# Four direct pairs in every feed-forward, and groups of seven products begun earlier

## The chip, the cores and the metric

The kernel runs on one core of one Trainium2 chip (trn2). The metric is the device time of one execution in microseconds (us), as the median of several runs. The engines of a core run side by side, each with its own queue in order: TensorE (PE in the profile, with PEld for its weight loads) does the matrix products, VectorE (DVE) and ScalarE (ACT) do the elementwise work, GpSimd (POOL) here issues the transfers that add while they write, and SyncE (SP) issues the plain transfers.

## The reference

Two decoder layers over 512 tokens of width 1024, all in float32. Each layer has three residual parts, and the change lies in the first and third:

```python
def swiglu_ffn(x, g, w_in, w_out):
    h = rms_norm(x, g)
    gate, up = jnp.split(h @ w_in, 2, axis=-1)
    return (jax.nn.silu(gate) * up) @ w_out
...
    for layer in range(DEPTH):
        x = x + 0.5 * swiglu_ffn(x, ffn1_norm[layer], ffn1_w_in[layer], ffn1_w_out[layer])
        # layer 0: retention and dilated attention; layer 1: stick-breaking attention
        ...
        x = x + 0.5 * swiglu_ffn(x, ffn2_norm[layer], ffn2_w_in[layer], ffn2_w_out[layer])
    return rms_norm(x, final_norm)
```

`D_FF` is 2816, so `w_in` has 22 column blocks of 128 for the gate and 22 for the up half, and `w_out` has 22 row blocks. There are four feed-forwards, called FFN0 to FFN3 below.

## The kernel before

**Precision.** A float32 product is made of three products of the short type fp32r. Every operand is split into `hi`, its rounded value, and `lo`, what is left. Then `hi*hi`, `hi*lo` and `lo*hi` are added up in PSUM. `split` (L224) makes the two with one ScalarE cast (L225) and one VectorE subtraction (L226). Where the source still lies in device memory there is a second way: ScalarE writes `-hi` into the `lo` buffer, and a transfer from POOL's queue adds the source to it. It is `weight_dma` (L194, with `minus_hi`, L189, its transfer is L192) for direct weights, and `cut_raw` (L468; cast L471, negation L472, transfer L473) for the blocks of a group.

**Two ways to do the first product.** A feed-forward's 22 gate and up blocks are done partly in *direct pairs* and partly in *groups of seven products*. A direct pair is one gate and one up block: 48 matmuls with 512 columns (8 row blocks, three fp32r products, gate and up). A group covers two gate and two up blocks by Winograd's form of Strassen's scheme: seven products of half the rows and half the tokens where the plain way needs eight. Each product is 24 matmuls with 256 columns. How many pairs are direct is `DIRECT`, one number for each feed-forward (L32); before, it is 6, 4, 4, 6, and the rest are 8, 9, 9 and 8 groups. `lazy` (L547) is true where it is 4: then the direct weights from the third pair on take `weight_dma`, the token forms are made one by one as the groups ask for them (a Python generator, `normed_forms`, L420), and buffers are dealt out differently.

**A group** is `quad` (L493). It loads four blocks a21, a11, a22, a12 of 512 KB (L497). The weight side of its products is, in order: p3, the sum of a11 and a21 (L499); p1, an addition in a21's buffer (L507); a22; a11; p2, an addition in a22's buffer (L513); p4, an addition in a11's buffer (L517); a12. The token sides are the forms T3, T1, T4, B11, T2, B22 and B21. Products T3 and T4 go into one PSUM bank one after the other, T1 and B22 into a second, B11 and B21 into a third, T2 into a fourth. Between T3 and T4 ScalarE has to copy the bank out (L505). The evictions after T2 are L522, L524 and L526, after B22 the addition L529, a silu and a product (L533), after B21 another silu and L533.

**Buffers.** Tiles come from numbered slots that are handed out in the order of the program, each role in a ring. While the groups run, the loaded blocks (`wraw`) have 7 slots for 4 blocks a group, the splits (`whl`) have 10 slots, that is five products' `hi` and `lo`, and p3 has one. So the split of a product can begin when the product five places ahead of it in the ring has been done. The first group of a feed-forward inherits the slots of the direct pairs in the order in which those were used.

**Order.** TensorE's instructions keep the order of the program by explicit edges (`ordered`, L119). The other engines' orders are laid out ahead by a scheduler that walks through modelled time: whenever an engine is free it takes, of the instructions that are ready in that model, the one written earliest. Once laid out, each queue runs strictly in order on the chip. So where a piece of code stands in the program decides which slots it gets and who goes first when two are ready.

**Around it.** Ahead of the direct pairs the norm's scale is finished by `norm_r` and `rstd` (ln and exp on ScalarE, then three VectorE instructions, L244, L245, L247), and everything that comes after the direct products needs it: the evictions of the pairs (L580, L587, L590), the normed activations (L429), their sums (L446) and the splits of the forms (L225 and L226). After the groups comes the second product (`out_ffn` or `out_last`).

Of the kernel before, what the change touches and what calls it, by code (L numbers as in the profile page):

```python
# [25 lines left out]
FC = DFF // P  # L26
# [2 lines left out]
NEG = -1.0e30  # L29
NORM_EPS = 1e-6  # L30
GN_EPS = 1e-5
DIRECT = (6, 4, 4, 6)  # L32


@with_exitstack
def trunk(ctx: ExitStack, tc: tile.TileContext, a: dict, out: bass.AP):
    nc = tc.nc
# [24 lines left out]
    def others():  # L62

        return [i for i in range(10, NSLOT) if i not in home["h"]]
# [13 lines left out]
    def B(shape, dt, tag):  # L78
        slot = roles[tag][turn_of[tag] % len(roles[tag])]
        turn_of[tag] += 1  # L80
        return big.tile(list(shape), dt, tag=f"m{slot}", name=nm(tag), bufs=1)
# [7 lines left out]
    def ATT():  # L89
        return PS("att")  # L90

    def f32(ap):
        return ap.bitcast(F32)
# [31 lines left out]
    def mm(*args, **kw):  # L125
        return ordered(nc.tensor.matmul(*args, **kw))  # L126
# [97 lines left out]
    def split(hi, lo, src):  # L224
        nc.scalar.copy(out=hi, in_=src)  # L225
        nc.vector.tensor_tensor(out=lo, in0=src, in1=f32(hi), op=ALU.subtract)  # L226
# [241 lines left out]
    def cut_raw(raw, src):  # L468

        hi, lo = (B((P, 2, SEQ), F32R, "whl") for _ in range(2))  # L470
        nc.scalar.copy(out=hi, in_=raw)  # L471
        nc.scalar.mul(out=lo, in_=f32(hi), mul=-1.0)  # L472
        nc.gpsimd.dma_start(lo, src, accum_op=ALU.add)  # L473
        return hi, lo

    def cut_form(src):
        hi, lo = (B((P, 2, SEQ), F32R, "whl") for _ in range(2))
        split(hi, lo, src)
        return hi, lo

    def product(bank, w, form, first):

        for p in range(2):
            o = bank[:, p * HT:p * HT + HT]
            for k in range(4):
                col = slice(k * P, k * P + P)
                h, l = (t[:, p, col] for t in w)
                bh, bl = form[k // 2][:, 0, k % 2, :], form[k // 2][:, 1, k % 2, :]
                mm(o, h, bh, start=first and p == 0 and k == 0, stop=False, skip_group_check=True)
                mm(o, h, bl, start=False, stop=False, skip_group_check=True)  # L490
                mm(o, l, bh, start=False, stop=k == 3, skip_group_check=True)

    def quad(wq, fm, uq, early, lazy):  # L493

        a21, a11, a22, a12 = (B((P, 2, SEQ), F32, "wraw") for _ in range(4))
        for t, i in ((a21, 2), (a11, 0), (a22, 3), (a12, 1)):
            nc.sync.dma_start(t, wq[i])  # L497
        p3 = B((P, 2, SEQ), F32, "p3")
        nc.vector.tensor_add(out=p3, in0=a11, in1=a21)  # L499
        if early and lazy:  # L500
            w22 = cut_raw(a22, wq[3])
        bc, bd_, ba, bb = (ATT() for _ in range(4))
        product(bc, cut_form(p3), next(fm)["T3"], True)
        s7 = T()
        nc.scalar.copy(out=s7, in_=bc)  # L505
        p1 = a21
        nc.vector.tensor_add(out=p1, in0=a21, in1=a22)  # L507
        product(bd_, cut_form(p1), next(fm)["T1"], True)
        w75 = T()
        nc.vector.tensor_add(out=w75, in0=bd_, in1=s7)  # L510
        w = (w22 if lazy else cut_form(a22)) if early else cut_raw(a22, wq[3])
        p2 = a22
        nc.vector.tensor_add(out=p2, in0=p1, in1=a11)  # L513
        product(bc, w, next(fm)["T4"], False)
        w = cut_form(a11) if early else cut_raw(a11, wq[0])
        p4 = a11
        nc.vector.tensor_add(out=p4, in0=p2, in1=a12)  # L517
        product(ba, w, next(fm)["B11"], True)
        u2 = T()
        nc.scalar.copy(out=u2, in_=ba)  # L520
        product(bb, cut_form(p2), next(fm)["T2"], True)
        nc.vector.tensor_add(out=u2, in0=bb, in1=u2)  # L522
        x21 = T(tag="tp")
        nc.vector.tensor_add(out=x21, in0=bc, in1=u2)  # L524
        x22 = w75
        nc.vector.tensor_add(out=x22, in0=u2, in1=w75)  # L526
        product(bd_, cut_form(p4), next(fm)["B22"], False)
        s2 = u2
        nc.vector.tensor_add(out=s2, in0=bd_, in1=u2)  # L529
        func(s2, s2, AF.Silu)  # L530

        def put(h, up, s):
            nc.vector.scalar_tensor_tensor(out=uq[:, :, h * HT:h * HT + HT], in0=up.rearrange("p (a t) -> p a t", a=2),  # L533
                                           scalar=-1.0, in1=s.rearrange("p (a t) -> p a t", a=2),
                                           op0=ALU.mult, op1=ALU.mult)

        put(1, x22, s2)
        product(ba, cut_raw(a12, wq[1]), next(fm)["B21"], False)
        s1 = T(tag="tp")
        func(s1, ba, AF.Silu)  # L540
        put(0, x21, s1)

    def ffn_seven(i, rms, gcol, first=None):

        order["on"] = True
        nd, wd, wq = DIRECT[i], a[f"wd{i}"], a[f"wq{i}"]
        lazy = nd == 4  # L547
        rest, old = others(), home["h"]
        forms, ext, late = rest[:14], rest[14:18], rest[18:]
        for i, n in enumerate(("T3", "T1", "T4", "B11", "T2", "B22", "B21")):  # L550
            give(**{"f" + n: forms[2 * i:2 * i + 2]})
        give(uq=late + old[:4])
        if lazy:
            give(wraw=oldest("wraw") + ext[:1], whl=oldest("whl") + ext[2:])
        uqs = []
        for f in range(nd):
            pg = ACC()
            if f == 0 and first:
                pu = ATT()
                for k in range(KC):  # L560
                    for w, ps in zip(first, (pg, pu)):
                        mm3(ps, w, k * P, hh[k][:, 0, :], hh[k][:, 1, :], k == 0, k == KC - 1)
            elif f == 0:
                with tc.high_priority(offset=FIRST):
                    w2 = [weight(wd[n], D) for n in (0, nd)]
                proj_tile(None, pg, w2[0])
            else:
                w2 = [(weight_dma if lazy and f >= 2 else weight)(wd[n], D) for n in (f, nd + f)]
                proj_tile(None, pg, w2[0])
            if f == 0 and first:  # L570
                rr = rms()
                act_set(SILU)
            elif f == 0:
                pu = ATT()
                for k, _ in enumerate(proj_steps(None, pu, w2[1])):
                    if k == 6:
                        rr = rms()
                        act_set(SILU)
            t1 = T(tag="tp")
            nc.vector.tensor_mul(out=t1, in0=pg, in1=rr)  # L580
            s = T()
            func(s, t1, AF.Silu)
            if f:
                pu = ATT()
                proj_tile(None, pu, w2[1])
            t2 = T(tag="tp")
            nc.vector.tensor_mul(out=t2, in0=pu, in1=rr)  # L587
            if f % 2 == 0:
                uqs.append(B((P, 2, SEQ), F32, "uq"))
            nc.vector.tensor_mul(out=uqs[-1][:, f % 2, :], in0=t2, in1=s)  # L590
        if lazy:
            fm = normed_forms(rr, gcol, late[nd // 2 + 1:], forms[12:] + forms[10:12])
            give(wraw=oldest("wraw") + old[6:], p3=ext[1:2], whl=oldest("whl") + old[4:6])
        else:
            fm = normed_forms(rr, gcol, ext, late[nd // 2:])
            for _ in range(7):
                next(fm)
            give(wraw=oldest("wraw") + ext[:3], p3=ext[3:], whl=oldest("whl") + old[4:])
        for q in range((FC - nd) // 2):
            uqs.append(B((P, 2, SEQ), F32, "uq"))  # L600
            quad(wq[q], fm, uqs[-1], q == 0, lazy)
        order["on"] = False
        ring, raws = oldest("whl"), oldest("wraw")
        give(u=forms + [i for i in raws + ring if i not in WSLOTS] + roles["p3"])
        us = []
        for f in range(FC):
            u = B((P, 2, SEQ), F32R, "u")
            split(u[:, 0, :], u[:, 1, :], uqs[f // 2][:, f % 2, :])
            us.append(u)
        give(wraw=[i for i in raws if i in WSLOTS], whl=[i for i in ring if i in WSLOTS])  # L610
        home["h"] = (late + old[:4])[:8]
        return us
# [478 lines left out]
    for c in range(KC):  # L1091
# [3 lines left out]
        if c % 2 == 0:  # L1095
            for i, (raw, _) in enumerate(first):
                sl = slice(c * P, (c + 2) * P)
                nc.sync.dma_start(raw[:, sl], a["wd0"][i * DIRECT[0]][:, sl])
    for c in range(KC):
# [83 lines left out]
def _layout(i):  # L1183
# [20 lines left out]
    for n in range(4):  # L1204
        c = cols(g(("ffn1", "ffn2")[n % 2] + "_w_in")[n // 2])
        nd = DIRECT[n]
        nq = (FC - nd) // 2
# [56 lines left out]
```

## Time and profile before

| what | value |
|---|---|
| median of 3 runs | 1921.74 us (1921.35 to 1922.25) |
| the profiled execution | 1922.35 us, of it 1920.6 us from the first to the last instruction |
| TensorE (PE) | 1902.4 us busy, 11694 matmuls |
| TensorE weight loads (PEld) | 1712.6 us |
| VectorE (DVE) | 1327.0 us, 1876 instructions |
| ScalarE (ACT) | 1048.5 us, 1500 instructions |
| GpSimd (POOL) | 156.7 us, 274 instructions |
| device memory | 162 GB/s over the span |

In the rows of a timeline the first column is the start of a group of like instructions in us from the span's start, the second its length, then engine, line, operation, output and inputs, shapes, the count, and in brackets how long the engine had been idle and what ended that. A matmul's length in these rows contains its way through the array and overlaps the next one; the distance from start to start is what it costs in a row of matmuls. A row of a table by windows has the window, its length, and the busy time of each engine with its count. In the chain of waits each row is a start, a length, and the work or wait that the end of the span was waiting for at that time.

### The profile page before, as it was taken

To read this page: it belongs to the slowest core of one execution; us is meant where nothing else is said; L and a number is where in the kernel's file an instruction comes from. 1 tells how busy PE (TensorE), PEld (TensorE's weight loads), DVE (VectorE), ACT (ScalarE), POOL (GpSimd) and SP (SyncE) were. 2 spreads that over 40 slices of the span, in tenths; PEclk is the share of its full clock that TensorE was granted. 3 is DMA by queue.
4 is the path that set the end of the run, shared out by engine and by line. 5 is a ranking of instruction groups with operands and counts; after the bars stand their busy time and mean duration, and the time that the engine had idled before them with its cause. 6 is when DMAs were issued, how large, how long until landed. Compare 5 with 4: busy or idle time off the path is not lost.

```text
span 1920.6 us, 29933 instructions
## 1 busy us (share of the span) xinstructions
PE 1902.4 (99%) x11694; PEld 1712.6 (89%) x11694; DVE 1327.0 (69%) x1876; ACT 1048.5 (55%) x1500; POOL 156.7 (8%) x274
## 2 busy tenths in 40 slices
PE   9999999999999999999999999999999999999998
PEld 7999988888888899998889999888888888999887
DVE  8867854478976976674587767453888878777534
ACT  6466732435676656663366667342666644666422
POOL 0011000011000011100001110000222200111000
PEclk9999999999999999999999999999999999999999
DMA  5477676574433677668867776777555443866432
GB/s 197 136 199 171 150 255 229 189 206 136 115 106 112 156 168 198 165 174 295 281 155 192 166 187 159 258 263 228 168 173 162 131 140 100 206 163 164 116 92 92
DMA packets 105823, 333.81 MB, mean 174 GB/s; under 512 B 13009, under 2 KB 14673, under 8 KB 105681
## 3 DMA queue, kind: packets, MB, share of 16 engines
q1 hardware_dynamic: 90560, 277.10, 44.4%
q0 software_dynamic: 14976, 54.53, 16.5%
q8 instruction: 92, 1.51, 0.3%
q14 instruction: 51, 0.41, 0.1%
q10 hardware_dynamic: 144, 0.26, 0.0%
HBM read 273.12 MB, written 37.75 MB: 162 GB/s over the span
## 4 chain that ended last, share of the span: by engine, by line
PE 89%; DVE 5%; DMA 2%; issue 1%; ACT 1%; POOL 0%; SPq 0%; DVEq 0%; ACTq 0%; POOLq 0%
PE acc L126 44%; PE att L126 43%; PE po L126 2%; DMA wraw<-wq 1%; DVE whl L226 1%; PE att L129 1%; ACT t L108 0%; POOL t L970 0%; DVE h L257 0%; DVE t L987 0%; DMA cut_sb_q<-whl 0%; ACT whl L225 0%; DMA cut_sb_v<-whl 0%; DVE ss L265 0%; DVE p L499 0%
## 5 line engine op out<-in xcount | busy, mean ns | idle before, releaser
L225 ACT CAST whl<-wraw 128x1024 fp32r<-128x1024 f32 (+4 forms) x320 | 315.0, 991 | 446.9 <-PE acc L126 201.3
L226 DVE TENSOR_TENSOR whl<-wraw,whl 128x1024 fp32r<-128x1024 f32 (+4 forms) x320 | 367.1, 1153 | 246.8 <-ACT whl L225 211.1
L126 PE MATMUL acc<-u,whl 128*128 128x512 f32 (+1 forms) x2178 | 481.3, 383 | 0.9 <-DVE whl L226 0.9
L126 PEld LDWEIGHTS acc<-u,whl 128*128 128x128 f32 x2178 | 400.1, 188 | 80.8 <-DVE whl L226 1.3
L126 PE MATMUL att<-fT,whl 128*128 128x256 f32 x3264 | 403.6, 283 | 3.5 <-ACT t L505 2.6
L126 PEld LDWEIGHTS att<-fT,whl 128*128 128x128 f32 x3264 | 396.9, 192 | 4.7 <-ACT t L505 3.2
L126 PE MATMUL att<-fB,whl 128*128 128x256 f32 x2448 | 305.1, 283 | 0.1
L126 PEld LDWEIGHTS att<-fB,whl 128*128 128x128 f32 x2448 | 298.7, 192 | 0.3 <-DVE whl L226 0.3
L126 PE MATMUL acc<-h,whl 128*128 128x512 f32 x1152 | 277.9, 392 | 1.4 <-DVE h L257 0.8
L126 PEld LDWEIGHTS acc<-h,whl 128*128 128x128 f32 x1152 | 214.6, 188 | 48.5 <-DVE h L257 2.2
L471 ACT CAST whl<-wraw 128x1024 fp32r<-128x1024 f32 x96 | 100.7, 1049 | 91.8 <-PE att L126 90.3
L473 POOL DMA_DIRECT2D whl<-wq x96 | 83.3, 868 | 757.8 <-ACT whl L472 468.2
L126 PE MATMUL att<-h,whl 128*128 128x512 f32 x480 | 115.0, 392 | 0.0
L126 PEld LDWEIGHTS att<-h,whl 128*128 128x128 f32 x480 | 90.1, 188 | 19.9 <-issue 1.4
L472 ACT ACTIVATE whl<-whl 128x1024 fp32r<-128x1024 f32 x96 | 101.8, 1060 | 2.8
L226 DVE TENSOR_TENSOR whl<-p,whl 128x1024 fp32r<-128x1024 f32 x34 | 41.7, 1225 | 74.9 <-ACT whl L225 74.9
L326 DVE SCALAR_TENSOR_TENSOR x<-acc,x 128x512 f32<-128x512 f32 (+1 forms) x33 | 22.3, 675 | 75.0 <-PE acc L126 75.0
L126 PE MATMUL acc<-whl,h 128*128 128x256 f32 x576 | 74.0, 284 | 0.0
L126 PEld LDWEIGHTS acc<-whl,h 128*128 128x128 f32 x576 | 71.8, 191 | 0.9
L108 ACT ACTIVATE t<-t 128x512 f32<-128x512 f32 (+1 forms) x98 | 56.0, 590 | 15.5 <-DVE t L529 12.8
L226 DVE TENSOR_TENSOR u<-uq,u 128x512 fp32r<-128x512 f32 x88 | 57.4, 688 | 10.1 <-ACT u L225 9.7
L499 DVE TENSOR_TENSOR p<-wraw,wraw 128x1024 f32<-128x1024 f32 x34 | 41.7, 1226 | 28.7 <-DMA wraw<-wq 27.9
(177 smaller groups left out, 2126.1 us busy)
## 6 DMA issues: line engine op xcount, KB each, us to landing
wraw<-wq SPq DMA_DIRECT2D x136, 512.0 KB, 5.1
whl<-wq POOLq DMA_DIRECT2D x96, 512.0 KB, 6.8
wraw<-f_out SPq DMA_DIRECT2D x66, 448.0 KB, 4.4
wraw<-wd SPq DMA_DIRECT2D x38, 512.0 KB, 3.7
wraw<-f_out SPq DMA_DIRECT2D x33, 512.0 KB, 4.5
cut_sb_q<-whl SPq DMA_DIRECT2D x16, 512.0 KB, 3.6
cut_sb_k<-whl SPq DMA_DIRECT2D x16, 512.0 KB, 3.8
cut_sb_v<-whl SPq DMA_DIRECT2D x16, 512.0 KB, 3.4
```

The lines of the kernel that those rows point to most:

```text
L108: r = nc.scalar.activation(out=o, in_=i, func=f, **kw)
L126: return ordered(nc.tensor.matmul(*args, **kw))
L129: return ordered(nc.tensor.transpose(*args, **kw))
L225: nc.scalar.copy(out=hi, in_=src)
L226: nc.vector.tensor_tensor(out=lo, in0=src, in1=f32(hi), op=ALU.subtract)
L326: nc.vector.scalar_tensor_tensor(out=x[d][:, sl], in0=ps[:, sl], scalar=0.5, in1=x[d][:, sl], op0=ALU.mult, op1=ALU.add)
L471: nc.scalar.copy(out=hi, in_=raw)
L472: nc.scalar.mul(out=lo, in_=f32(hi), mul=-1.0)
L473: nc.gpsimd.dma_start(lo, src, accum_op=ALU.add)
L499: nc.vector.tensor_add(out=p3, in0=a11, in1=a21)
```

## The change

`DIRECT` becomes 4, 4, 4, 4, so that FFN0 and FFN3 also have four direct pairs and nine groups, and are `lazy`. The head of `quad` becomes a function of its own, `quad_begin`: the four loads, the addition p3 and its split, in the first group the split of a22 by `cut_raw`, the addition p1 and its split. It is called once ahead of the groups, and then inside each `quad` for the group behind it, after the additions that follow T2 and ahead of product B22 and the evictions of B22 and B21. The split of a12 also moves, from just ahead of product B21 to just ahead of that call. In the first group the three splits of `quad_begin` now take their slots in the order p3, a22, p1, where before it was a22, p3, p1.

```diff
-DIRECT = (6, 4, 4, 6)
+DIRECT = (4, 4, 4, 4)
...
-    def quad(wq, fm, uq, early, lazy):
+    def quad_begin(wq, early):
 
         a21, a11, a22, a12 = (B((P, 2, SEQ), F32, "wraw") for _ in range(4))
         for t, i in ((a21, 2), (a11, 0), (a22, 3), (a12, 1)):
             nc.sync.dma_start(t, wq[i])
         p3 = B((P, 2, SEQ), F32, "p3")
         nc.vector.tensor_add(out=p3, in0=a11, in1=a21)
-        if early and lazy:
-            w22 = cut_raw(a22, wq[3])
+        w3 = cut_form(p3)
+        w22 = cut_raw(a22, wq[3]) if early else None
+        p1 = a21
+        nc.vector.tensor_add(out=p1, in0=a21, in1=a22)
+        return a11, a22, a12, p1, w3, cut_form(p1), w22
+
+    def quad(wq, fm, uq, early, lazy, begun, begin):
+
+        a11, a22, a12, p1, w3, w1, w22 = begun
         bc, bd_, ba, bb = (ATT() for _ in range(4))
-        product(bc, cut_form(p3), next(fm)["T3"], True)
+        product(bc, w3, next(fm)["T3"], True)
         s7 = T()
         nc.scalar.copy(out=s7, in_=bc)
-        p1 = a21
-        nc.vector.tensor_add(out=p1, in0=a21, in1=a22)
-        product(bd_, cut_form(p1), next(fm)["T1"], True)
+        product(bd_, w1, next(fm)["T1"], True)
         w75 = T()
         nc.vector.tensor_add(out=w75, in0=bd_, in1=s7)
-        w = (w22 if lazy else cut_form(a22)) if early else cut_raw(a22, wq[3])
+        w = w22 or (cut_form(a22) if early else cut_raw(a22, wq[3]))
...
-        product(bd_, cut_form(p4), next(fm)["B22"], False)
+        w4, w12 = cut_form(p4), cut_raw(a12, wq[1])
+        begun = begin()
+        product(bd_, w4, next(fm)["B22"], False)
...
-        product(ba, cut_raw(a12, wq[1]), next(fm)["B21"], False)
+        product(ba, w12, next(fm)["B21"], False)
...
+        return begun
...
-        for q in range((FC - nd) // 2):
+        nq = (FC - nd) // 2
+        begun = quad_begin(wq[0], lazy)
+        for q in range(nq):
             uqs.append(B((P, 2, SEQ), F32, "uq"))
-            quad(wq[q], fm, uqs[-1], q == 0, lazy)
+            begun = quad(wq[q], fm, uqs[-1], q == 0, lazy, begun,
+                         lambda: quad_begin(wq[q + 1], False) if q < nq - 1 else None)
```

## The prediction, on record before the changed kernel was run

> **What bounds the kernel now.** I read the page first: busy times, then the chain that ended last.
>
> ```profile
> PE 1902.4 (99%) x11694; PEld 1712.6 (89%) x11694; DVE 1327.0 (69%) x1876; ACT 1048.5 (55%) x1500; POOL 156.7 (8%) x274
> ...
> PE 89%; DVE 5%; DMA 2%; issue 1%; ACT 1%; POOL 0%; SPq 0%; DVEq 0%; ACTq 0%; POOLq 0%
> ```
>
> TensorE is busy 99% of the span, and the chain runs through it for 89%. So the change can win in two ways: fewer or shorter matmuls, and the few places where the chain leaves TensorE. First the matmuls, in the table by windows: one direct pair of FFN0, then one group of FFN0.
>
> ```profile
> 30.19:41.07 10.88, 10.88 (x49) 9.01 (x48) 1.00 0.30 95
> 73.71:93.86 20.15, 20.15 (x169) 20.14 (x168) 1.00 0.56 142
> ```
>
> Both windows are full. A pair costs 10.88 us, a group, which does the work of two pairs, 20.15 us, that is 2.88 us for each of its seven products. Next, where TensorE waits. I asked for its waits in the groups of each feed-forward: FFN0, FFN2 and FFN3 have none, all lie in the first three groups of FFN1. Its timeline there:
>
> ```profile
> 653.66 5.91 PE L126 MATMUL att<-fT,whl 128*128 128x256 f32 x48
> 660.80 3.14 PE L126 MATMUL att<-fT,whl 128*128 128x256 f32 x24 [1.23 <-ACT t L505]
> ...
> 669.54 6.29 PE L126 MATMUL att<-fB,whl 128*128 128x256 f32 x48
> 675.66 5.92 PE L126 MATMUL att<-fT,whl 128*128 128x256 f32 x48
> 682.42 3.13 PE L126 MATMUL att<-fT,whl 128*128 128x256 f32 x24 [0.84 <-ACT t L505]
> ...
> 697.97 6.01 PE L126 MATMUL att<-fT,whl 128*128 128x256 f32 x48 [0.90 <-DVE t L522]
> 704.55 3.13 PE L126 MATMUL att<-fT,whl 128*128 128x256 f32 x24 [0.57 <-ACT t L505]
> ...
> 719.04 1.24 PE L126 MATMUL att<-fT,whl 128*128 128x256 f32 x9
> ```
>
> The first three groups start at 653.66, 675.66 and 697.97, the fourth at 719.04: 65.4 us where three undisturbed groups take 60.45, so 4.9 us are lost. The chain in that stretch says why:
>
> ```profile
> 616.11 1.15 DVE whl L226
> 617.25 0.02 issue
> 617.27 10.20 DMA wraw<-wq
> ...
> 627.57 1.23 DVE p L499
> 628.79 0.61 DVE t L244
> ...
> 668.78 1.23 DVE whl L226
> 670.00 0.02 issue
> 670.02 4.54 DMA wraw<-wq
> ...
> 674.69 1.23 DVE p L499
> ```
>
> VectorE's queue has the first group's addition p3 (L499) ahead of the norm's scale (L244). It waits for a load that took 10.20 us, so the scale and all that follows begin at 628.79, 24.9 us ahead of the groups. Later the third group's p3 waits for a slot that the split of p4 frees at 670.0, and evictions stand behind it.
>
> **The change part by part.** *Two pairs become a group, in FFN0 and FFN3.* 2 x 10.88 - 20.15 = 1.61 us less each, 3.2 us together, all on the path, as TensorE has no gap there. By the Trainium skill (TensorE: Matmul & The Clock Gate, Back-to-back issue gap) a matmul of N columns costs N/2.4 + 2.5 ns, which would make a pair 10.36 us, a group 18.35 us and the gain 4.7 us. The windows show 10.88 and 20.15, so the measurement decides, and the sum goes on with 3.2.
>
> *FFN0 and FFN3 become lazy, with 22 us less ahead of the groups.* VectorE loses eight weight splits in each (two pairs gone, two moved to POOL's transfers) and ScalarE trades casts for negations; both lie beside TensorE. The question is whether the forms are ready. These rows give the scale's start (L244) and the first group's start for FFN0, FFN2 and FFN3.
>
> ```profile
> 22.30 0.68 DVE L244 SCALAR_TENSOR_TENSOR t<-po,t 128x512 f32<-128x512 f32 x1
> 73.71 8.80 PE L126 MATMUL att<-fT,whl 128*128 128x256 f32 x72
> ...
> 972.28 1.23 DVE L499 TENSOR_TENSOR p<-wraw,wraw 128x1024 f32<-128x1024 f32 x1 [6.67 <-DMA wraw<-wq]
> 974.37 0.69 DVE L244 SCALAR_TENSOR_TENSOR t<-po,t 128x512 f32<-128x512 f32 x1 [0.86 <-ACT t L108]
> 1005.34 8.80 PE L126 MATMUL att<-fT,whl 128*128 128x256 f32 x72
> ...
> 1575.38 0.68 DVE L244 SCALAR_TENSOR_TENSOR t<-po,t 128x512 f32<-128x512 f32 x1
> 1627.44 8.80 PE L126 MATMUL att<-fT,whl 128*128 128x256 f32 x72
> ```
>
> FFN2, lazy already, has 31.0 us between the two and loses nothing; FFN1 has 24.9 and loses 4.9. Less 21.76, FFN0 will have 29.7 and FFN3 30.3: on FFN2's side. But both get a p3 addition that the scheduler can put ahead of L244 or into the forms' row, as in FFN1. I take 0.5 us each, 1.0 together, near FFN2; the bounds are 0 and 4.9 each. The four subtracting transfers that each gains go to POOL's queue, where the code puts nothing else at that time.
>
> *The first group's slots.* This is the part with teeth. Before, the splits came as a22, p3, p1; now as p3, a22, p1. Five products later p4 inherits p3's slot (free after T3) instead of a22's (free after T4), and a12 inherits a22's instead of p3's. ACT's and POOL's rows in FFN2 show the old order, those of a later group the way from cast to transfer, and the last row all such transfers:
>
> ```profile
> 1008.30 1.05 ACT L471 CAST whl<-wraw 128x1024 fp32r<-128x1024 f32 x1 [1.93 <-PE att L126]
> 1009.25 0.58 ACT L505 COPY t<-att 128x512 f32<-128x512 f32 x1
> ...
> 1011.15 0.86 POOL L473 DMA_DIRECT2D whl<-wq  x1 [18.26 <-PE att L126]
> ...
> 1014.06 1.05 ACT L225 CAST whl<-wraw 128x1024 fp32r<-128x1024 f32 x1 [1.21 <-PE att L126]
> ...
> 1111.98 1.05 ACT L471 CAST whl<-wraw 128x1024 fp32r<-128x1024 f32 x1 [1.35 <-PE att L126]
> ...
> 1114.47 0.86 POOL L473 DMA_DIRECT2D whl<-wq  x1 [7.77 <-ACT whl L472]
> ...
> DMA to landing us min/median/max: 5.4/6.8/9.3
> ```
>
> a12's cast (1008.30) waited for T3, 2.96 us after the group's start at 1005.34; p4's (1014.06) for T4, at 8.72. Now a12's cast starts at 8.72, its transfer 2.49 us later at 11.2, and it lands at 18.0 with the median of 6.8. B21 starts at 6 x 2.88 = 17.28, and its third matmul, at 17.5, is the first to use `lo`. So TensorE waits 0.5 us in the first group of all four feed-forwards: 2.0 us. Bounds: 5.4 lands at 16.6, no wait; 9.3 lands at 20.5, 3.0 us each, 12 in all. Behind that transfer POOL holds only the next group's.
>
> *FFN1's 4.9 us.* p3's wait ahead of L244 stays. But p4's split moves up; how far is set by its addition (L517):
>
> ```profile
> 661.70 1.22 DVE L517 TENSOR_TENSOR wraw<-wraw,wraw 128x1024 f32<-128x1024 f32 x1
> ...
> 1008.14 1.22 DVE L517 TENSOR_TENSOR wraw<-wraw,wraw 128x1024 f32<-128x1024 f32 x1
> ```
>
> In FFN1 the addition ends at 662.9; cast and subtraction bring the split's end to about 665.3 instead of 670.0, and the load behind it starts that much earlier, so the wait at 674.69 mostly goes. The cast of a12 also no longer stands ahead of the copy L505 on ScalarE, worth 1.0 of the first 1.23 us. I take 2.4 us of the 4.9: that 1.0, the 0.4 lost inside B22 (from 669.54 to 675.66 are 6.12 us for two products), and 1.0 of the rest, because what is late next is the row of loads itself. Bounds: 4.9 less, or 3.8 more if p4's cast is put ahead of L505 (662.9 + 1.0 + 0.6 = 664.5 for a copy that T4 needs at 659.4 and now gets at 660.8).
>
> *The groups behind the first.* VectorE's row of the group around 1114.47, with the next group's work ahead of the eviction of T2:
>
> ```profile
> 1115.93 1.23 DVE L226 TENSOR_TENSOR whl<-p,whl 128x1024 fp32r<-128x1024 f32 x1 [3.08 <-ACT whl L225]
> 1117.20 1.23 DVE L499 TENSOR_TENSOR p<-wraw,wraw 128x1024 f32<-128x1024 f32 x1
> ...
> 1120.81 0.69 DVE L522 TENSOR_TENSOR t<-att,t 128x512 f32<-128x512 f32 x1
> ```
>
> The split of p3 and the additions stand ahead of the evictions already, since they are ready first. Writing them earlier changes nothing; 0. Bounds: with no waits there, no gain; a loss if an eviction slips behind a late split: L529 has two products, 5.8 us, and p1's addition and two subtractions of 1.22 us (the length of L517) take 3.7. SP issues the same loads in the same slot order.
>
> **The sum.** -3.2 + 1.0 + 2.0 - 2.4 = -2.6 us against the profiled execution's 1922.35 us, 1919.75. The median shown is 0.61 us below that execution, so the forecast is 1919.1 us.
>
> **The rivals.** *A faster one: the a12 transfers land in time and FFN1's waits nearly go.* For it: 5.4 us transfers exist, and the late loads are one chain that starts at p4's split. -3.2 + 0.5 - 4.9 = -7.6, that is 1914.1 us. By the Trainium skill (DMA: Bandwidth & Descriptors, Anatomy of one DMA — SWDGE (gpsimd) path) such a transfer takes 2.0 us plus its bytes over 436 GB/s, 3.2 us for 512 KB, which would make this rival's first half certain; the row above with its least of 5.4 does not agree.
>
> *The reordering does nothing:* FFN1 keeps its 4.9 us, only the 2.0 of a12 comes: -1.2, 1920.5 us. For it: the steady state's order; against it: the slots do change.
>
> *A slower one: FFN0 and FFN3 inherit FFN1's wait*, p3 ahead of L244 behind a load that shares the engines with a subtracting transfer. In FFN3 the load's slot comes free next to the first such transfer, as in FFN1. -3.2 + 2 x 4.9 + 2.0 = +8.6, 1930.3 us; with FFN3 alone +3.7, 1925.4. It decides once the scale starts less than about 26 us ahead of the groups. Against it: FFN2 has the same code and p3 was done at 973.5, before L244 was due.
>
> **How the numbers follow.** Forecast 0.43, faster rival 0.23, no effect 0.18, slower rival 0.16. A difference of 0.2%, 3.8 us, is about what a measurement of this kernel can tell from none: under 1917.9 or over 1925.6. Faster: the 0.23 and 0.08 of the forecast's lower side, 0.31. Slower: most of the 0.16, 0.14. The same: 0.55. The range is 1914.0, the faster rival's time, to 1927.0, which holds FFN3's wait alone and leaves out both together. The forecast case's own range is 1916 to 1923.
>
> **What would show it.** Right: groups of 20.15 us in FFN0 and FFN3, each a pair-for-group exchange; in each first group a wait of B21 for POOL's transfer, and p4's cast right after T3; FFN1's first group under 21.5 us. Wrong: L499 with an idle of several us ahead of L244 in FFN0 or FFN3, with waits on L505 behind it; or no wait at B21; or new waits in later groups, where I expect none.

## The result, and the profile after

The changed kernel takes 1927.39 us (median of 10 executions, 1924.12 to 1930.96); the kernel before took 1921.88 us beside it (10 executions, 1919.31 to 1923.66). The ratio is 1.0026, 95% interval 1.0018 to 1.0034: slower by a quarter of a per cent, 8.3 us above the forecast and 0.4 us above its range. The profiled execution took 1924.67 us with a span of 1923.0, so it is 2.7 us faster than its own median. Both differences need an explanation: the 2.3 us between the two traces, and the rest that this trace does not hold.

The busy times of the changed kernel (share of the span, number of instructions), and TensorE's waits by what ended them (us in total, number of waits, the longest):

```profile
PE 1900.7 (99%) x11838; PEld 1718.1 (89%) x11838; DVE 1326.0 (69%) x1876; ACT 1072.0 (56%) x1526; POOL 170.2 (9%) x290
```

```profile
PE att L126 <- DMA whl<-wq: 5.2, 4, 2.1
PE acc L126 <- DVE whl L226: 2.2, 2, 1.6
...
```

TensorE's busy time fell by 1.7 us and the span rose by 2.4, so its idle time rose by 4.1. The first line is new: before, no matmul waited for a transfer of `wq`. A window over a later group of FFN0 and one over a later group of FFN3 (the columns behind the window are its length, the busy time of PE, PEld, DVE, ACT and POOL with their instructions, the granted clock, the share of the DMA engines, and GB/s):

```profile
77.78:97.94 20.16, 20.16 (x171) 20.16 (x170) 16.34 (x19) 12.91 (x15) 2.04 (x3) 1.00 0.71 173
1650.10:1670.26 20.16, 20.16 (x170) 20.16 (x170) 14.18 (x16) 12.50 (x15) 2.58 (x4) 1.00 0.76 184
```

Both are full and as long as predicted. So the exchange of pairs for groups works; what is lost is lost in the first groups. By the starts of the groups, the first one of FFN0, FFN1, FFN2 and FFN3 takes 4.8, 2.4, 1.6 and 0.5 us more than 20.16, and every group behind a first one takes 20.16. TensorE's timeline of the first group in FFN0, FFN1, FFN2 and FFN3:

```profile
52.79 3.27 PE L126 MATMUL att<-fT,whl 128*128 128x256 f32 x26
56.92 2.90 PE L126 MATMUL att<-fT,whl 128*128 128x256 f32 x22 [0.86 <-DVE whl L226]
60.21 3.13 PE L126 MATMUL att<-fT,whl 128*128 128x256 f32 x24 [0.39 <-ACT t L512]
...
70.28 3.25 PE L126 MATMUL att<-fB,whl 128*128 128x256 f32 x25 [1.07 <-DVE fB L226]
75.05 2.89 PE L126 MATMUL att<-fB,whl 128*128 128x256 f32 x22 [1.51 <-DMA whl<-wq]
...
657.50 8.79 PE L126 MATMUL att<-fT,whl 128*128 128x256 f32 x72
...
671.89 3.28 PE L126 MATMUL att<-fB,whl 128*128 128x256 f32 x26
677.32 2.90 PE L126 MATMUL att<-fB,whl 128*128 128x256 f32 x22 [2.14 <-DMA whl<-wq]
...
1026.44 2.90 PE L126 MATMUL att<-fB,whl 128*128 128x256 f32 x22 [1.32 <-DMA whl<-wq]
...
1627.01 2.90 PE L126 MATMUL att<-fB,whl 128*128 128x256 f32 x22 [0.26 <-DMA whl<-wq]
```

The groups start at 52.79, 657.50, 1007.45 and 1609.08. In all four, B21 stops after its first two matmuls (x26 is the 24 of B22 and two more) until POOL's transfer of a12 has landed. The idle times are 1.51, 2.14, 1.32 and 0.26 us; from start to start of the two matmuls, less the usual 0.12, each costs 0.16 more, 5.9 us together. FFN0 also has three waits that it did not have, 2.8 us counted in the same way. FFN1's old waits are gone: T3, T1 and T4 run there as one row of 72 matmuls. ScalarE and POOL in FFN1's first group show how a12 became late:

```profile
665.12 1.05 ACT L225 CAST whl<-wraw 128x1024 fp32r<-128x1024 f32 x1 [3.16 <-DVE wraw L522]
666.33 1.05 ACT L225 CAST whl<-p 128x1024 fp32r<-128x1024 f32 x1 [0.16 <-PE att L126]
667.29 1.04 ACT L471 CAST whl<-wraw 128x1024 fp32r<-128x1024 f32 x1
...
669.91 0.86 POOL L473 DMA_DIRECT2D whl<-wq  x1 [15.82 <-DVE whl L226]
```

The casts stand in the order p4 (waiting for its addition, L522), p3 of the next group, a12. T4 is done 8.7 us into the group, at 666.2, but a12's cast (L471) starts at 667.29, behind the begun group's p3. The transfer is issued 12.4 us into the group and lands 7.4 us later, where B21 needs it at 17.5.

### The profile page after: what moved, and what is told of

It is laid out like the page before. It is cut to its first block, busy times and chain, and to the rows that moved or that the text cites. A ratio compares the mean times of both kernels' runs of the same rounds, so it can differ in the third digit from the quotient of the medians.

```text
span 1923.0 us, 30296 instructions
## 1 busy us (share of the span) xinstructions
PE 1900.7 (99%) x11838; PEld 1718.1 (89%) x11838; DVE 1326.0 (69%) x1876; ACT 1072.0 (56%) x1526; POOL 170.2 (9%) x290
## 5 line engine op out<-in xcount | busy, mean ns | idle before, releaser
L226 DVE TENSOR_TENSOR whl<-wraw,whl 128x1024 fp32r<-128x1024 f32 (+4 forms) x308 | 352.9, 1150 | 243.5 <-ACT whl L225 206.0
L126 PE MATMUL att<-fT,whl 128*128 128x256 f32 x3456 | 427.0, 283 | 1.2 <-DVE whl L226 0.9
L126 PEld LDWEIGHTS att<-fT,whl 128*128 128x128 f32 x3456 | 420.3, 192 | 2.0 <-DVE whl L226 1.1
L126 PE MATMUL att<-fB,whl 128*128 128x256 f32 x2592 | 324.1, 284 | 6.3 <-DMA whl<-wq 5.2
L126 PEld LDWEIGHTS att<-fB,whl 128*128 128x128 f32 x2592 | 316.5, 192 | 7.3 <-DMA whl<-wq 6.0
L126 PE MATMUL acc<-h,whl 128*128 128x512 f32 x1056 | 256.3, 394 | 0.9 <-DVE whl L226 0.6
L126 PEld LDWEIGHTS acc<-h,whl 128*128 128x128 f32 x1056 | 196.9, 188 | 44.6 <-DVE h L257 2.2
L471 ACT CAST whl<-wraw 128x1024 fp32r<-128x1024 f32 x104 | 109.1, 1049 | 99.3 <-PE att L126 99.3
L126 PE MATMUL att<-h,whl 128*128 128x512 f32 x384 | 92.9, 394 | 0.0
L126 PEld LDWEIGHTS att<-h,whl 128*128 128x128 f32 x384 | 72.6, 189 | 16.4 <-issue 1.4
L326 DVE SCALAR_TENSOR_TENSOR x<-acc,x 128x512 f32<-128x512 f32 (+1 forms) x33 | 22.3, 675 | 76.6 <-PE acc L126 76.6
L981 POOL TENSOR_SCALAR_AFFINE_SELECT t<-t 128x128 f32<-128x128 f32 x128 | 45.5, 377 | 186.7 <-DVE t L998 121.6
```

Of the source, the lines that this page charges most:

```text
L326: nc.vector.scalar_tensor_tensor(out=x[d][:, sl], in0=ps[:, sl], scalar=0.5, in1=x[d][:, sl], op0=ALU.mult, op1=ALU.add)
L981: nc.gpsimd.affine_select(out=t[:, at:at + P], in_=t[:, at:at + P], pattern=[[1, P]], compare_op=ALU.is_gt, fill=0.0, base=0, channel_mult ...
```

## The experiments

Unless another is named, the edits stand against the changed kernel. Times are medians; each ratio is against executions of the kernel before on the same chip, where that kernel took 1922.15, 1922.65 and 1922.40 us in the three sets of four.

**direct_only: the four direct pairs alone.** The kernel before, with one line changed.

```diff
-DIRECT = (6, 4, 4, 6)
+DIRECT = (4, 4, 4, 4)
```

> The kernel before with DIRECT = 4, 4, 4, 4 and nothing else: quad as it was. Slot theory: no waits of B21 anywhere; two groups for four pairs give 3.2 us; FFN1 keeps its 4.9 us; FFN0 waits 2 to 5 us, since its first loads stand beside the four new subtracting transfers and VectorE waits for them; median 1919 to 1924. Crowding rival: B21 waits in FFN0 and FFN3 as in the changed kernel (about 2 us), 1922 to 1927.

1922.70 us, ratio 1.0002 (0.9994 to 1.0011): no difference. TensorE's waits in the groups of its trace, all of them in FFN0, FFN1 and FFN3 and none at B21:

```profile
PE att L126 <- ACT t L505: 3.0, 5, 0.9
...
PE att L126 <- DVE whl L226: 0.8, 1, 0.8
```

By the starts of the groups FFN0 loses 3.5 us and FFN3 1.1, which is more than the 3.2 us of shorter matmuls. FFN1, which lost 4.9 us in the trace of the kernel before and is the same code here, loses 2.6, against the expectation; so its loss is not a fixed one.

**begin_only: the early beginning alone.** The changed kernel with the old direct pairs.

```diff
-DIRECT = (4, 4, 4, 4)
+DIRECT = (6, 4, 4, 6)
```

> The changed kernel with DIRECT = 6, 4, 4, 6: only the earlier beginning, with its slot order p3, a22, p1 in the lazy FFN1 and FFN2. Slot theory: B21 waits in FFN1 and FFN2 alone, 1.3 to 2.3 us each, none in FFN0 and FFN3, where a22 is not split by a transfer in the first group; FFN1's old 4.9 us go; together 1 us less than the kernel before, 1919 to 1922. Crowding rival (four lazy feed-forwards needed): no waits of B21, 4 to 5 us less than before, 1917.

1923.97 us, ratio 1.0011 (1.0002 to 1.0020). FFN0 and FFN3 have no wait here; FFN1 has a single one, of 3.31 us, at B21 for a12. FFN2 has none, against the expectation: its transfer of a12 is issued 11.2 us into the group, but took 6.4 us. Windows of this trace around FFN1's wait:

```profile
672.27:675.68 3.41, 1.24 (x10) 1.24 (x11) 3.31 (x6) 1.20 (x2) 1.41 (x2) 1.00 0.83 141
675.68:679.09 3.41, 3.41 (x18) 3.41 (x18) 2.42 (x3) 1.38 (x2) 0.00 (x0) 0.50 1.03 203
679.09:682.50 3.41, 3.41 (x31) 3.41 (x29) 1.83 (x2) 1.68 (x3) 0.00 (x0) 1.00 0.82 219
```

No theory had this up to here: behind the wait the granted clock is 0.50 for 3.41 us, in which TensorE issues 18 matmuls where the next window holds 31. The missing 13 are 13/31 of 3.41 us, 1.4 us on top of the wait.

**a22_first and a22_third: the order of the first group's slots.** The split of a22 goes ahead of p3's, as in the kernel before (first diff), or behind p1's (second).

```diff
+        w22 = cut_raw(a22, wq[3]) if early else None
         w3 = cut_form(p3)
-        w22 = cut_raw(a22, wq[3]) if early else None
```

```diff
         w3 = cut_form(p3)
-        w22 = cut_raw(a22, wq[3]) if early else None
         p1 = a21
         nc.vector.tensor_add(out=p1, in0=a21, in1=a22)
-        return a11, a22, a12, p1, w3, cut_form(p1), w22
+        w1 = cut_form(p1)
+        w22 = cut_raw(a22, wq[3]) if early else None
+        return a11, a22, a12, p1, w3, w1, w22
```

> The changed kernel with the slot order of the kernel before: quad_begin makes its splits in the order a22, p3, p1. Slot theory: B21's waits go (under 0.5 us), but p4 is back on the slot that T4 frees, so its split, and the loads and p3 additions behind it, are late again: FFN1 gets back 2 to 5 us of waits on the bank copy and on evictions, FFN0 gets 2 to 5 us too, FFN2 none; median about 1921 to 1925. Crowding rival: B21 keeps at least 4 us of waits.

a22_first: 1925.70 us, ratio 1.0022 (1.0011 to 1.0032). No first group waits for a12, as the slot theory wants, yet the ratio does not differ from the changed kernel's by what these runs can tell. TensorE's waits in its trace:

```profile
PE att L126 <- ACT t L512: 4.0, 5, 1.3
...
PE att L126 <- DVE whl L226: 1.5, 2, 0.9
```

Most of these lie in FFN0. By the starts of the groups FFN0 loses 5.6 us, with a wait of 0.64 us for a12 in its second group among them, FFN3 1.9 and FFN1 1.1, less than the 2 to 5 us expected there. p4's split is among what is late. The old order moves the lateness from a transfer to the bank copy (L512) and to splits.

> The changed kernel with one edit: quad_begin makes its splits in the order p3, p1, a22 instead of p3, a22, p1, so in a first group a12 inherits the slot that comes free after T1, as in every later group. Slot theory (the changed kernel's waits of B21 come from a12 inheriting the slot that T4 frees): B21's waits for POOL's transfer, 5.9 us in the four first groups of the changed kernel's profile, fall under 0.5 us in all; FFN1 stays without other waits; FFN0's own 2.8 us stay; the median falls by 5 to 7 us, to about 1921. Crowding rival (four lazy feed-forwards have so many transfers in flight that a12's is late whatever its slot): at least 4 us of the waits stay, and the median stays within 2 us of the changed kernel's.

a22_third: 1938.83 us, ratio 1.0087 (1.0074 to 1.0101), a clear miss of the expectation. TensorE and POOL in FFN3:

```profile
1616.38 6.15 PE L126 MATMUL att<-fT,whl 128*128 128x256 f32 x50
1626.56 4.39 PE L126 MATMUL att<-fT,whl 128*128 128x256 f32 x22 [4.02 <-DMA whl<-wq]
```

```profile
1618.03 0.86 POOL L473 DMA_DIRECT2D whl<-wq  x1 [15.15 <-ACT whl L472]
```

Here a22's own transfer is the late one. T4 stops after its first two matmuls (x50), because POOL issued the transfer only 1.65 us into the group; in the changed kernel it was issued 6.5 us ahead of it. a22 is third in the order here, so its slots come from a later direct product, and ScalarE's cast of it, at 1614.82, also stands behind casts of the forms; how much each of the two delays it was not tried. The row of 22 matmuls behind the wait takes 4.39 us instead of 2.90: the half clock again (0.50 from 1627.28 to 1630.69).

**a12_form: no transfer for a12 in the first groups.** ScalarE and VectorE split it instead.

```diff
-        w4, w12 = cut_form(p4), cut_raw(a12, wq[1])
+        w4, w12 = cut_form(p4), cut_form(a12) if early else cut_raw(a12, wq[1])
```

> The changed kernel, but in the first group of each feed-forward a12 is split by ScalarE and VectorE (as a11 is there) instead of by POOL's subtracting transfer. Transfer theory: the loss is TensorE's wait in B21 for that transfer (1.67, 2.30, 1.48 and 0.41 us in the profiled run, 5.9 together), and in executions where one wait is longer the clock is granted at half for 3.41 us behind it, as in the trace of begin_only (3.31 us idle, then 0.5 for 3.41 us), 1.7 us more. So all four waits go, the granted clock is 0.998 or 0.999 in every run, and the time is 1927.4 - 5.9 - about 2.7 (median less profiled run) = 1919. Lateness rival: the loss is that the four feed-forwards start with too little lead, VectorE above all; another split of 1.23 us on it in that stretch makes FFN0 and FFN1 wait more for L226, L503 and L512, and the time stays at 1924 or above.

1922.63 us, ratio 0.9998 (0.9989 to 1.0007). The waits for a12 are gone, and the trace has no half-clock window between the start and the end. Against the changed kernel's ratio the gain is 0.28%, 5.4 us, of the 8.4 expected. About half of it is the clock's: the changed kernel's median lies 2.7 us above its trace, this kernel's median is that of its trace. The waits themselves gained less, for by the starts of the groups the first ones still lose 7.5 us here instead of 9.3. As the rival said, other waits came in place of those for a12, for VectorE and for the bank copy:

```profile
PE acc L126 <- DVE whl L226: 2.8, 2, 2.1
PE att L126 <- DVE fB L226: 2.2, 1, 2.2
PE att L126 <- ACT t L512: 2.1, 3, 1.0
```

**ffn0_six: six direct pairs in FFN0.**

```diff
-DIRECT = (4, 4, 4, 4)
+DIRECT = (6, 4, 4, 4)
```

> The changed kernel with six direct pairs in FFN0 and four in the others. FFN0's late start as a lazy feed-forward costs 2.8 us of waits for its forms and splits and 1.67 for a12 in the profiled run, and saves 1.61. Lateness theory: without it the time falls by 2.8 + 1.7 - 1.6 = 2.9 us to 1924.5, more if FFN0 is also where the clock drops. Transfer theory alone (FFN0's waits are those of its transfer, the others give back elsewhere): FFN0's 1.67 against 1.61, no change, 1927.

1927.03 us, ratio 1.0023 (1.0014 to 1.0032), no change. But not for the reason of the second theory: FFN0 has no wait left, and FFN1's and FFN3's waits for a12 grew to 3.61 and 3.14 us, each with a half-clock window behind it:

```profile
1625.12:1628.54 3.42, 0.28 (x3) 0.27 (x3) 3.42 (x4) 2.96 (x3) 0.94 (x2) 1.00 0.58 90
1628.54:1631.95 3.41, 3.41 (x18) 3.41 (x18) 3.31 (x5) 0.63 (x1) 0.79 (x1) 0.50 0.94 197
```

In FFN3 a12's transfer is now issued 13.9 us into the group instead of 11.2, since VectorE's queue there reaches p4's addition later and ScalarE's casts follow it in order. Ahead of that, p3's addition waited 8.02 us for its load, and the norm's scale came 25.6 us ahead of the groups instead of 29.4. So what FFN0 gained FFN1 and FFN3 lost. That the edit did this is not shown: one of the further executions of the changed kernel below (after_c) has the same late scale in FFN3.

**begin_late: the next group begun at the end of the group.**

```diff
-        begun = begin()
...
-        return begun
+        return begin()
```

> The changed kernel with the next group begun at the end of the group (behind B21's evictions) instead of ahead of B22; slots as in the changed kernel. Transfer theory: in FFN1 the next group's p3 split no longer goes ahead of a12's cast on ScalarE, so that transfer is issued at 11.2 us into the group instead of 12.4, its wait falls from 2.30 to about 1.1 us, and the rest stays: 1926, within 1.5 us of the changed kernel. Rival, that beginning ahead of the evictions is what removed FFN1's other waits: 2 to 5 us of waits on L512 and L529 come back in the groups behind the first, and the time is 1929 or above.

1934.47 us, ratio 1.0061 (1.0049 to 1.0074): as slow as the rival had it, by a mechanism that neither named. No wait on L512 or L529 came back in the groups behind the first, and none of FFN1's old waits in its first group; so they can go without the early call. B21 waits 1.60, 2.92, 0.41 and 5.04 us for a12. ScalarE in FFN1 and FFN3:

```profile
670.06 1.05 ACT L225 CAST whl<-p 128x1024 fp32r<-128x1024 f32 x1 [2.73 <-DVE p L499]
671.01 1.05 ACT L472 ACTIVATE whl<-whl 128x1024 fp32r<-128x1024 f32 x1
...
1623.68 1.05 ACT L225 CAST whl<-p 128x1024 fp32r<-128x1024 f32 x1 [3.10 <-DVE p L499]
1624.64 1.04 ACT L471 CAST whl<-wraw 128x1024 fp32r<-128x1024 f32 x1
```

The cast of the next group's p3 still stands ahead of a12's cast in FFN3, and between a12's cast (at 666.28) and its negation in FFN1. Now p3's addition comes later on VectorE, so ScalarE stands idle for 2.73 and 3.10 us with a12's instructions behind it. This shows the second half of a12's lateness: ScalarE works in order, and the begun group is in front.

**swap: a12's split ahead of p4's, so that a12 inherits T3's slots.**

```diff
-        w4, w12 = cut_form(p4), cut_raw(a12, wq[1])
+        w12, w4 = cut_raw(a12, wq[1]), cut_form(p4)
```

> The changed kernel with a12 split before p4, so that a12 inherits the slots that T3 frees and p4 those that T4 frees: the slots' part of the change undone with one line, everything else kept. Slot theory (a12's transfer is late because of the slot, its price 5.9 us of waits and the clock's drops behind them): a12's transfer is issued 6 to 9 us into the first groups instead of 11.2 to 16.3, B21 waits for nothing, the granted clock is 0.998 or 0.999; 1927.4 - 5.9 - 2.0 = 1919.5, with up to 3 us of waits for evictions instead, as in a12_form: 1919 to 1923. Rival, that a12's transfer is late because ScalarE has the next group's split ahead of it: the transfer is still issued at 10 us or later in FFN0 and FFN1, and the time stays above 1925.

> The same with six direct pairs in FFN0. Slot theory: as swap without FFN0's waits (2.8 us against the 1.61 that two more pairs cost), so 1 to 3 us below swap: 1918 to 1920, beside six_form. Rival: above 1924.

swap: 2057.22 us, ratio 1.0714 (1.0697 to 1.0732); six_swap, with six pairs in FFN0: 2051.61 us, 1.0684 (1.0658 to 1.0711). Both are far outside what was expected. The first groups do what the slot theory says: a12's transfer is issued 9.1, 6.8, 5.8 and 7.1 us into them, and none waits for it at B21. But the new order holds in every group. A later group of FFN2 on TensorE, its a11 on POOL, and TensorE's waits in swap:

```profile
1135.46 8.80 PE L126 MATMUL att<-fT,whl 128*128 128x256 f32 x72
1144.10 0.40 PE L126 MATMUL att<-fB,whl 128*128 128x256 f32 x2
1147.35 2.93 PE L126 MATMUL att<-fB,whl 128*128 128x256 f32 x12 [2.85 <-DMA whl<-wq]
```

```profile
1138.39 0.86 POOL L473 DMA_DIRECT2D whl<-wq  x1 [5.23 <-ACT whl L472]
```

```profile
PE att L126 <- DMA whl<-wq: 78.2, 29, 4.5
```

The slots after the exchanged pair have other owners, and a11's transfer now starts 2.9 us into the group that needs it at 8.9. 29 waits of 2.7 us (78.2 together) and 19 stretches of half clock make most of the 118 us by which this trace is longer than that of the kernel before (the median is 135 us longer).

**form_6446 and before_6444: which half pays.** The first is a12_form with the old direct pairs (6, 4, 4, 6); the second the kernel before with pairs (6, 4, 4, 4). **six_form** is a12_form with (6, 4, 4, 4).

> Both edits: six direct pairs in FFN0, and a12 split by ScalarE and VectorE in the first groups. If the two costs add: 1924.5 - the 4.2 us of a12's waits in the other three feed-forwards - what the clock's drops cost there (up to 2.7) = 1917.6 to 1920.3, faster than the kernel before (1922). If VectorE's additional splits are late instead: 1922 or above.

> The early beginning and a12's split on ScalarE and VectorE, with the direct pairs of the kernel before (6, 4, 4, 6). If FFN3's exchange of two pairs for a group is worth its 1.61 us less the 1.4 us of new waits that six_form's trace shows there: 1919.2 + 0.2 = 1919.4, no difference from six_form. If those waits would be there anyhow: 1920.8.

> The kernel before with four direct pairs in FFN3 too, and six in FFN0. FFN3 gives 1.61 us and keeps most of the gain: direct_only's trace has 0.8 us of waits there. 1922.2 - 1.6 + 0.8 = 1921.4. A rival, that lazy feed-forwards lose what they save: 1922.2 or above.

six_form: 1919.16 us, ratio 0.9983 (0.9974 to 0.9992). form_6446: 1919.72 us, 0.9987 (0.9978 to 0.9996). before_6444: 1924.04 us, 1.0010 (1.0001 to 1.0019). The first two beat both kernels, by less than 0.2% against the one before; they do not differ from each other by what these runs can tell. So one more lazy feed-forward brings no gain that can be measured with the early beginning, and without it a small loss, as before_6444's rival had it. The gain is FFN1's: in form_6446's trace every group of FFN0, FFN2 and FFN3 takes 20.15 or 20.16 us, as in the kernel before. FFN1's first group there, as a window:

```profile
653.32:673.50 20.18, 20.18 (x170) 20.17 (x169) 20.18 (x25) 11.72 (x14) 1.19 (x2) 1.00 0.56 168
```

TensorE is full, the next two groups start 20.16 and 40.60 us behind it, and of the 4.9 us only 0.3 are left. VectorE is busy for all of the 20.18 us: there is no room for another split.

**after_b and after_c: the changed kernel again.**

> The changed kernel as it is, one more execution with a trace. Clock theory: its executions differ by whether B21's wait for a12 puts 1.9 us or more of TensorE's idle time into one window of 3.41 us. In the trace of the changed kernel FFN1's 2.14 us fell on both sides of a window's border (1.21 and 0.93) and the clock stayed. Here either one wait lies within one window and the clock is 0.50 in the next (mean granted clock 0.997 or less, time 1926 to 1930), or none does and the time is 1923 to 1926. A rival, that the slower executions only have longer waits: 1927 or more with no half-clock window behind the start.

> The same again: the clock theory ties the time to the number of half-clock windows behind the start, 1.4 us for each beside the wait itself; the rival to the length of the waits alone.

1927.23 and 1927.63 us, both at the median, with 4.8 and 7.1 us idle at B21, on either side of the first trace's 5.2. Both have two half-clock windows between the start and the end, the first trace has none. Two windows each of the first trace, of after_b and of after_c, and the one behind the wait ahead of FFN1's down projection in after_c:

```profile
672.97:676.39 3.42, 2.21 (x19) 2.00 (x17) 3.42 (x4) 2.99 (x4) 0.86 (x1) 1.00 0.80 146
676.39:679.80 3.41, 2.48 (x20) 2.48 (x21) 3.31 (x5) 0.60 (x1) 0.88 (x1) 1.00 1.06 167
```

```profile
676.34:679.76 3.42, 1.36 (x12) 1.16 (x11) 3.42 (x5) 2.04 (x2) 1.74 (x2) 1.00 0.91 144
679.76:683.17 3.41, 3.41 (x19) 3.41 (x18) 2.77 (x4) 1.10 (x2) 0.00 (x0) 0.50 1.01 244
```

```profile
672.97:676.38 3.41, 1.46 (x12) 1.47 (x13) 3.41 (x5) 1.19 (x2) 1.30 (x2) 1.00 0.82 123
676.38:679.79 3.41, 3.41 (x18) 3.41 (x18) 2.48 (x4) 1.76 (x3) 0.00 (x0) 0.50 1.04 220
905.08:908.49 3.41, 1.33 (x7) 0.79 (x5) 3.18 (x5) 2.26 (x4) 0.00 (x0) 1.00 0.94 333
908.49:911.90 3.41, 3.41 (x8) 2.72 (x9) 0.89 (x1) 0.00 (x0) 0.00 (x0) 0.50 0.99 321
```

FFN1's wait is about the same in the first two (2.14 and 2.06 us). In the first trace it fell on both sides of a border, 1.21 and 0.93 us, and the clock stayed; in after_b it lay in one window and the clock fell. TensorE's idle time is nearly the same in the three traces, 22.3, 22.1 and 22.9 us, while its busy time is 2.7 and 2.3 us longer in the two new ones; so the rival, longer waits alone, does not hold. Two windows at 1.4 us are 2.8 us, against the 2.6 and 3.0 us by which these executions are above the first. That is the rest of the loss, as far as three traces show it.

The waits themselves change from execution to execution. B21 waits for a12 in four first groups of the first trace and of after_c, but in two of after_b, where the transfers of FFN2 and FFN3 took 5.6 and 5.5 us. In FFN3 p3's addition, ahead of L244, waited 4.17, 5.11 and 7.83 us for its load in the first trace, after_b and after_c. In after_c the scale then came 25.8 us ahead of the groups, a12's transfer was issued 13.7 us into the group, and FFN3 lost 2.1 us instead of 0.5.

## Why the prediction was wrong

Term by term, for the profiled execution; the measured column is from the trace of the changed kernel.

| term | predicted, us | measured, us |
|---|---|---|
| two pairs become a group, twice | -3.2 | -3.2 |
| FFN0 and FFN3 lazy | +1.0 | +2.8, all in FFN0 |
| a12's transfer at B21 | +2.0 | +5.9 |
| FFN1's old waits | -2.4 | -4.9 |
| later groups | 0 | 0 |
| not in the sum: FFN1's down projection waits 1.73 instead of 1.07 | | +0.7 |
| not in the sum: the first 20 us | | +0.8 |
| sum | -2.6 | +2.1 (+2.3 by the two times) |

The measured waits are counted by their idle time and 0.16 us each. By the starts of the groups the first groups lose 0.6 us more than the two terms hold, and the stretches from FFN0's groups to FFN1's and from FFN2's to FFN3's are together 0.5 us shorter than the terms have them.

**The step that failed is a12's term**, at 5.9 instead of 2.0 us, inside its bound of 12 but three times the value taken. The slot was right: in FFN2 and FFN3 the transfer is issued 11.2 us into the group, as worked out. What the prediction left out is that ScalarE takes its casts in order. In FFN1 the next group's p3 stands ahead of a12's cast (issued at 12.4 us), in FFN0, where p4's addition is late too, it is issued at 16.3. Not all of the 3.9 us is this: FFN2's cast came on time, and its wait of 1.48 us instead of 0.5 is that of a transfer of 7.7 us. The prediction costed the early beginning at nothing for the later groups and was right there; the price was in the same group, on the queue that a12 shares with what was begun. The two transfers issued at 11.2 us took 7.7 and 6.7 us where I had taken 6.8.

**The lateness of FFN0 was the second.** I read it from the 29.7 us between the norm's scale and the groups and put it beside FFN2. The lead came out as said, 30.3 us, but not all of it could be used. VectorE in FFN0:

```profile
22.52 0.69 DVE L244 SCALAR_TENSOR_TENSOR t<-po,t 128x512 f32<-128x512 f32 x1 [1.15 <-ACT t L108]
...
33.90 1.23 DVE L499 TENSOR_TENSOR p<-wraw,wraw 128x1024 f32<-128x1024 f32 x1 [4.71 <-DMA wraw<-wq]
...
38.75 1.23 DVE L503 TENSOR_TENSOR wraw<-wraw,wraw 128x1024 f32<-128x1024 f32 x1 [2.37 <-DMA wraw<-wq]
```

p3 and p1 stand in the middle of the forms, and VectorE is idle for 7.1 us waiting for their loads. The term named both places for p3, ahead of L244 or in the forms' row, and took 0.5 us for it; the slower rival priced only the first, and here it came in the second. That these waits make the 2.8 us was not tried by an edit. The changed kernel's three traces bear it out: in after_b p3 waits 4.24 us and TensorE's three waits are there again (0.36, 0.40 and 1.06 us), in after_c p3 waits 2.32 us and a single wait of 0.23 us is left. In FFN3 p3 did come ahead of L244, with a wait of 4.17 us, and cost nothing in this trace: 29.4 us of lead were left, above the 26 that the rival named. That was luck in part: in after_c the lead was 25.8 us and FFN3 lost 2.1 us. So the slower rival's condition can be met, at less than half of its price, and the loss then came at B21 for a12 and not on the bank copy.

**FFN1's term was wrong in the other direction.** All of the 4.9 us went. begin_late, which has the new slots without the early call, has none of the old waits either, so p4's inheritance of T3's slot can be enough for them. But a22_first, with the early call and the old slots, loses only 1.1 us in FFN1, and direct_only, with neither, 2.6. The lead of the scale also grew, from 24.9 to 26.6 us. How the 4.9 us divide between these causes stays open.

**A loss that the sum had no term for.** The forecast set the median 0.6 us below the profiled execution. It lies 2.7 above. Two further executions, both at the median, pay for half-clock windows behind the new waits, which the trace of before, with no wait above 1.23 us in the groups, could not show.

The two halves of the change are nearly free apart (+0.02% and +0.11%) and cost 0.26% together; the 0.13% between is no more than the intervals of these ratios leave open. In the first trace the two together have four first groups that wait for a12, where begin_only has one, and FFN0's late chain in front of one of them.

## What to carry to other kernels

When work is begun early, ask on each in-order queue what now stands behind it: here a cast for the next group delayed the transfer that the present group needed first. Rotating slots tie every buffer to the release of an earlier one, so exchanging two lines in a loop can move each later transfer; follow the owners through a whole turn before counting a gain. And cost a wait on TensorE not only by its length: here a wait of 2 us or more was often followed by 3.41 us at half clock, which cost another 1.4 us.

## What the runs showed of the hardware

Between the start and the end of these traces TensorE's granted clock falls to 0.50 for exactly one window of 3.41 us, or for two of them, when the window just before had too little matmul work. In each trace all falls and rises lie whole multiples of 3.41 us apart, so the windows run on by themselves, and a wait counts by how it falls on their borders. Among the waits for a12 and its like the bound is narrow. A window of swap and the next, and one of begin_late and the next:

```profile
208.16:211.57 3.41, 1.56 (x14) 1.36 (x12) 1.76 (x2) 1.04 (x1) 0.00 (x0) 1.00 1.04 257
211.57:214.98 3.41, 2.93 (x24) 2.94 (x25) 0.14 (x1) 0.12 (x1) 0.00 (x0) 1.00 0.97 264
```

```profile
71.15:74.57 3.42, 1.53 (x10) 1.33 (x11) 3.42 (x4) 3.36 (x5) 0.85 (x1) 1.00 0.31 62
74.57:77.98 3.41, 3.41 (x18) 3.41 (x17) 3.41 (x6) 0.88 (x1) 0.89 (x2) 0.50 0.81 129
```

With 1.56 us of matmuls in a window at full clock the next stayed at 1.00, with 1.53 it fell, at 1.85 and 1.89 us of idle time. It is no rule in busy time alone: in six_swap a window with 1.61 us of matmuls of 512 columns (from 1390.16) fell, and so did one with 1.72 us near the end of the changed kernel's trace (from 1912.01). So between 1.7 and 1.9 us of idle time the clock went either way. In a window that is itself at half clock, less is enough: with 0.66 us of idle time or more the next one stayed at half (eight times in these traces), with 0.53 or less it went back to full. The Trainium skill (TensorE: Matmul & The Clock Gate, What's actually happening) gives the window as 3413 ns and free-running, and this case's traces agree. The same section puts the return to half clock after at least one idle window of about 3.4 us; here a window idle for 55% was enough, in begin_late made of the last 0.29 us of one wait and the 1.60 us of another, so the measurement decides.
